# Moving the matmul operands of a one-core decoder layer to other places in the on-chip memory

## The chip, the cores and the metric

The kernel runs on one core of a Trainium2 chip. The metric is the device time of one execution in microseconds (us), the median of several runs. A profiled execution gives a page and a trace; its span runs from the first to the last instruction of the core.

## The reference

One post-norm decoder layer over 272 tokens (16 meta tokens and 256 others), width 2048, float32:

```
p = h @ W_in            # q | latent | index q | index key | index weights | pool channels
attn = sparse attention over the latent (64 best keys of each query, chosen by the index)
pool = trailing means (2, 4, 8, 16) less the token, mapped by group and scaled
h = LN(alpha * h + concat(attn, pool) @ W_o)
z = h @ w_up            # 2048 -> 2 * 5632
z = causal convolution of width 3 over the tokens, plus a bias
f = (gelu(a) * g) @ w_down          # a, g: the halves of z
h = LN(alpha * h + f)
```

## The kernel before

**Two parts, three products.** Every float32 operand of a large product is split into an upper part (rounded by ScalarE to the engine's faster float32 format, float32r) and a lower part (what is left, by VectorE). A product of activation and weight is then three matmuls that add up in PSUM: weight upper by activation upper (line 258), weight upper by activation lower (line 259), weight lower by activation upper (line 260). `product` issues these three for each of 16 blocks of 128 rows, 48 matmuls for one tile of 128 output channels. In all of them the weight is the stationary operand (loaded, 128x128) and the activation the moving one (streamed, 256 to 272 columns, 258 in most). In the down projection it is the other way round: `seven` and the "down" items stream 512 columns of weight over a loaded block of activation (lines 855 to 857 and 907 to 909).

**The weight tiles.** Weights come in 1 MB tiles. SyncE fetches a tile into `wraw` (three buffers); `split_part` makes the upper part on ScalarE (line 149) and the lower on VectorE (line 150), in two pieces of 1024 columns, into `whl` (three buffers). `weights` hands out the next tile and keeps two more in flight. `stream` is the order of the tiles: index queries, latent maps, queries, pool channels, output map, then the plan of the feed-forward part, in which up tiles and down tiles alternate.

**The activation slots.** The activations' two parts lie in `ring`, 24 slots of the tag "act": first `xp` (the input, 16 slots), then `mixa` and `mixp` (the input of the output map), then `hp` (the normalised activations, read by 80 up tiles), and `right` (gated activations of the down projection). The first eight up tiles read `fold` instead, activations before the normalisation, in 16 buffers of the pool `ffn`, which later hold the gated activations `gp`.

**Where they lie.** Class `Split` says where the parts of a weight tile start, class `Parts` where those of a slot start:

```
self.tile, self.places = tile, ((0, 1040), (2080, 3120)) if sums else ((0, 1024), (2080, 3104))
self.parts = flat[:, 6:6 + NQ], flat[:, 280:280 + NQ]
```

All places are in elements of 4 bytes. A slot is 2 x 272 elements, 2176 bytes or 8.5 times 256, so that neighbouring slots lie 128 bytes apart modulo 256. In a slot of `hp`, `mixa` or `mixp` the upper part starts 24 bytes in and the lower 1120. A weight tile has 4160 elements, 65 times 256 bytes, and so the three `whl` buffers start at one place modulo 256 (96 in the built program). Its four pieces start at 0 or at 128 modulo 256 from there: upper and lower of the first eight blocks at 0, of the other eight at 128. A block of 128 columns is 512 bytes, so that all blocks of a piece have that place. The buffers of `fold` and `gp` are 2080 bytes apart, which gives eight places modulo 256, 32 bytes apart.

The order of the work is the program's own on each engine, with edges (`issue_after`) that place some of VectorE's and ScalarE's instructions behind the split of a later tile. The reserved area at the start of the on-chip memory, 16384 bytes of each partition, holds the descriptors of the transfers that GpSimd issues.

Of the kernel before, what the change touches and what calls it, by code (L numbers as in the profile page):

```python
# [11 lines left out]
F32 = mybir.dt.float32  # L12
F32R = mybir.dt.float32r
# [4 lines left out]
P = 128  # L18
# [3 lines left out]
T = NM + S  # L22
Q0 = NM - 2
NQ = T - Q0
# [43 lines left out]
class Split:  # L68

    def __init__(self, tile, sums):

        self.tile, self.places = tile, ((0, 1040), (2080, 3120)) if sums else ((0, 1024), (2080, 3104))

    def __getitem__(self, key):
        rows, part, c = key
        a, b = c.start, 2 * 1024 + 2 if c.stop is None else c.stop
        at = int(a >= 1024)
        assert b <= 1024 or at == 1  # L80
        o = self.places[at][part] - 1024 * at
        return self.tile[rows, o + a:o + b]


class Parts:


    def __init__(self, slot):
        flat = slot.rearrange("p a b -> p (a b)")
        self.parts = flat[:, 6:6 + NQ], flat[:, 280:280 + NQ]  # L90

    def __getitem__(self, key):
        return self.parts[key[1]][key[0], key[2]]

K_PROJ = (1, 3, 5, 7, 9, 11, 13, 15, 0, 2, 4, 6, 8, 10, 12, 14)
K_O = (1, 3, 5, 7, 9, 10, 12, 14, 0, 2, 4, 6, 8, 11, 13, 15)
K_UP = (1, 3, 5, 7, 8, 10, 12, 15, 0, 2, 4, 6, 9, 11, 13, 14)  # L100
# [3 lines left out]
def tile_layer(ctx, tc, xt, w_first, w_proj, w_uk, w_uv, w_pool, w_o, w_up, w_down, cols, rows, rel_bias, onehot, out):  # L104
    nc = tc.nc
    sb = ctx.enter_context(tc.tile_pool(name="sb", bufs=1))
    wp = ctx.enter_context(tc.tile_pool(name="wp", bufs=3))
    ring = ctx.enter_context(tc.tile_pool(name="ring", bufs=24))
# [17 lines left out]
    stream = [w_proj[j] for j in range(8)] + [w_uk, w_uv] + [w_proj[j] for j in range(8, 24)]  # L126
    stream += [w_o[j] for j in range(KT)]
    plan = ffn_plan()
    kinds = {}
    for item in plan:  # L130
        if item[0] == "up":
            stream.append(w_up[item[2] * FT + item[1]])
        elif item[0] == "down":
            n = PARTS[FAST]
            stream.append(w_down[sum(PARTS[:FAST]) + n // 2 + (item[2] - 1) // 2 * (n // 4) + item[3]])
        else:
            kinds[len(stream)] = item[0]
            stream.append(w_down[sum(PARTS[:item[1]]) + item[2] * (PARTS[item[1]] // 2) + item[3]])
    stream += [w_down[d] for d in range(FT - PARTS[-1], FT)]
    spare, last = len(stream) - PARTS[-1], len(stream) - 1  # L140
    VALUES = stream.index(w_uv)
    ready, raws, split, held = {}, {}, {}, []
    state = {"next": 0, "use": 0}
# [26 lines left out]
            parts = split_part(raw, hl, slice(a, b))  # L170
        return parts

    def split_tile(sums=False):

        hl = Split(wp.tile([P, 4160], F32R, tag="whl", name="whl"), sums)
        if not state["use"]:

            wp.tile([P, 16], F32, tag="gap", name="gap", bufs=1)
        return hl

    def weight_tiles(sums=False):
        raw = wp.tile([P, 2048], F32, tag="wraw", name="wraw")
        return raw, split_tile(sums)

    def emit(i):
        if i in ready:
            return
        if i == last:

            raw = wp.tile([P, 2048], F32, tag="wraw", name="wraw")  # L190
            nc.sync.dma_start(raw, stream[i])
            raws[i] = raw
            ready[i] = []
            for c in range(0, 2048, 256):
                hl = ring.tile([P, 2, 258], F32R, tag="act", name="whl_r", padded_shape=[P, 2, T])
                nc.scalar.activation(hl[:, 0, :256], raw[:, c:c + 256], AF.Copy)
                nc.vector.tensor_tensor(hl[:, 1, :256], raw[:, c:c + 256], hl[:, 0, :256].bitcast(F32), op=ALU.subtract)
                ready[i].append(hl)
            return
        if i == spare:  # L200
            raw = wp.tile([P, 2048], F32, tag="wraw", name="wraw")
            hl = Split(sb.tile([P, 4160], F32R, tag="y", name="whl_y"), True)
        else:
            raw, hl = weight_tiles(i > spare)
        ready[i] = hl
        if i == VALUES:

            nc.sync.dma_start(raw, stream[i])
            held.extend((raw, hl))
            return  # L210
        split[i] = fetch(raw, hl, stream[i], kinds.get(i), i and i - 1 in split and split[i - 1][1])
        if i >= spare:
            raws[i] = raw
# [48 lines left out]
    at = ctx.enter_context(ExitStack())  # L262
# [4 lines left out]
    for k0, k1 in [(k, k + 1) for k in range(9)] + [(9, 12), (12, 15), (15, 16)]:  # L267
        if k0 == KT - 1:

            raw = ap_.tile([P, 1024], F32, name="wraw_l", tag="v1")[:, :T + MF].rearrange("p (a b) -> p a b", a=1)  # L270
        elif k0 % 3 == 0:
            raw = wp.tile([P, 2048], F32, tag="wraw", name="wraw")
            raw = raw[:, :3 * (T + MF)].rearrange("p (a b) -> p a b", b=T + MF)
        if k0 % 6 == 0:
            hl = split_tile()
        for w in ((slice(0, T), slice(T, T + MF)) if k0 == 0 else (slice(0, T + MF),)):
            nc.sync.dma_start(raw[:, k0 % 3:k0 % 3 + k1 - k0, w], w_first[k0:k1, :, w].rearrange("k p c -> p k c"))
        for k in range(k0, k1):
            xk, wk, a0 = raw[:, k % 3, :T], raw[:, k % 3, T:], k % 6 // 3 * 1024 + k % 3 * MF
            c = slice(a0, a0 + MF)  # L280
            a = ring.tile([P, 2, T], F32R, tag="act", name="xp")
            nc.scalar.activation(a[:, 0, :], xk, AF.Copy)
            nc.scalar.activation(hl[:, 0, c], wk, AF.Copy)
            nc.vector.tensor_tensor(a[:, 1, :], xk, a[:, 0, :].bitcast(F32), op=ALU.subtract)
            nc.vector.tensor_tensor(hl[:, 1, c], wk, hl[:, 0, c].bitcast(F32), op=ALU.subtract)
            x_parts.append(a)
            first.append((hl, c.start))
# [143 lines left out]
    for j in range(8):  # L431
        hl = weights()
# [10 lines left out]
        for i in range(2):  # L443
            r, o = slice(DI * i, DI * i + DI), slice(DI - DI * i, 2 * DI - DI * i)
# [27 lines left out]
    y = sb.tile([P, KT, T], F32, tag="y", name="x", padded_shape=[P, KT, T])  # L472
# [50 lines left out]
    for h in range(H):  # L523
        hl = weights()
# [65 lines left out]
    def values(h, pts, ptx):  # L590
        ps = small()
        hs = slice(h * HD, (h + 1) * HD)
        nc.tensor.matmul(ps[:, :NQ], vs[0][:, hs], ptx, start=True, stop=False)
        nc.tensor.matmul(ps[:, 2:NQ], vs[1][:, hs], pts[:, :2 * P], start=False, stop=False)
        nc.tensor.matmul(ps[:, 2 + P:NQ], vs[2][:, hs], pts[:, 2 * P:], start=False, stop=True)
        a = Parts(ring.tile([P, 2, T], F32R, tag="act", name="mixa"))
        nc.scalar.activation(a[:, 0, :NQ], ps[:, :NQ], AF.Copy)
        nc.vector.tensor_tensor(a[:, 1, :NQ], ps[:, :NQ], a[:, 0, :NQ].bitcast(F32), op=ALU.subtract)
        mix[h] = a
# [33 lines left out]
    def pooled(g, df, hl):  # L633
        for j in range(2):
            ps = small()
            for c in range(2):
                w = slice(256 * c + j * P, 256 * c + j * P + P)
                nc.tensor.matmul(ps[:, :NQ], hl[:, 0, w], df[:, c, 0, :], start=c == 0, stop=False)
                nc.tensor.matmul(ps[:, :NQ], hl[:, 0, w], df[:, c, 1, :], start=False, stop=False)
                nc.tensor.matmul(ps[:, :NQ], hl[:, 1, w], df[:, c, 0, :], start=False, stop=c == 1)  # L640
            m = 2 * g + j
            a = Parts(ring.tile([P, 2, T], F32R, tag="act", name="mixp"))
            nc.scalar.activation(a[:, 0, :NQ], ps[:, :NQ], AF.Copy, scale=col(G_POOL, m))
            nc.vector.scalar_tensor_tensor(a[:, 1, :NQ], ps[:, :NQ], col(G_POOL, m), a[:, 0, :NQ].bitcast(F32),
                                           op0=ALU.mult, op1=ALU.subtract)
            mix[8 + m] = a
# [5 lines left out]
    for h in range(H):  # L652
# [3 lines left out]
        hl = weights()  # L656
# [47 lines left out]
    sums = fp.tile([P, NQ + W], F32, name="sums", tag="u1", bufs=1)  # L704
# [64 lines left out]
    def normalise(m):  # L769
        yd = y[:, m, Q0:]  # L770
        nc.vector.tensor_tensor(yd, yd, rs, op=ALU.mult)  # L771
        nc.vector.tensor_tensor(yd, yd, m2, op=ALU.add)
        nc.scalar.activation(yd, yd, AF.Identity, bias=col(LN1, 2 * m + 1), scale=col(LN1, 2 * m))
        a = Parts(ring.tile([P, 2, T], F32R, tag="act", name="hp"))
        nc.scalar.activation(a[:, 0, :NQ], yd, AF.Copy)
        nc.vector.tensor_tensor(a[:, 1, :NQ], yd, a[:, 0, :NQ].bitcast(F32), op=ALU.subtract)  # L776
        h_parts.append(a)
# [45 lines left out]
    def forms(r, j, whole):  # L823
# [6 lines left out]
        nc.gpsimd.tensor_tensor(s[:, 3], a11, a21, op=ALU.subtract)  # L830
        left = two_parts(slot(), r[:, :, :P])
        mid = two_parts(slot(), s[:, :2])
        right = ring.tile([P, 2, T], F32R, tag="act", name="right")
        right = two_parts(right[:, :, :2 * P].rearrange("p a (b c) -> p a b c", c=P), s[:, 2:])
        if j % 2 == 0:
            held["lone"], held["other"] = slot(), slot() if whole else None
# [52 lines left out]
    for item in plan:  # L889
# [3 lines left out]
        if item[0] == "down":  # L893
            _, part, c, g = item
            hl = weights()
# [6 lines left out]
            n = PARTS[part]  # L902
# [18 lines left out]
        hl = weights()  # L921
# [233 lines left out]
```

## Time and profile before

| what | value |
|---|---|
| time, median of 3 runs | 1034.75 us (1034.6 to 1035.13) |
| span of the profiled execution | 1032.8 us |
| TensorE matmul busy | 1025.7 us, 99% |
| VectorE busy | 890.4 us, 86% |
| ScalarE busy | 622.4 us, 60% |
| GpSimd busy | 187.0 us, 18% |
| mean granted TensorE clock | 0.997 |
| moved by DMA | 250.28 MB, 242 GB/s |

The three runs lie 0.5 us apart. The span is 2.0 us under their median; a run's time has, beside the span, what lies before the first and after the last instruction. Matmuls overlap in TensorE's pipeline: a matmul's own duration (some 280 ns) is far longer than the distance from its start to the start of the next, and the busy time says only that something was in flight. The distance from start to start, called the pitch below, is what adds up to the time; it is read by counting starts in a stretch.

### The profile page before, as it was taken

To read this page: it belongs to the slowest core of one execution; us is meant where nothing else is said; L and a number is where in the kernel's file an instruction comes from. 1 tells how busy PE (TensorE), PEld (TensorE's weight loads), DVE (VectorE), ACT (ScalarE), POOL (GpSimd) and SP (SyncE) were. 2 spreads that over 40 slices of the span, in tenths; PEclk is the share of its full clock that TensorE was granted. 3 is DMA by queue.
4 is the path that set the end of the run, shared out by engine and by line. 5 is a ranking of instruction groups with operands and counts; after the bars stand their busy time and mean duration, and the time that the engine had idled before them with its cause. 6 is when DMAs were issued, how large, how long until landed. Compare 5 with 4: busy or idle time off the path is not lost.

```text
span 1032.8 us, 19199 instructions
## 1 busy us (share of the span) xinstructions
PE 1025.7 (99%) x7644; PEld 977.2 (95%) x7644; DVE 890.4 (86%) x1401; ACT 622.4 (60%) x1000; POOL 187.0 (18%) x245
## 2 busy tenths in 40 slices
PE   9999999999999999999999999999999999999997
PEld 8999999999999999999999999999999999999986
DVE  6878668758779998889999999999998999998976
ACT  7666446645448865655665555656556565565675
POOL 1200014125430022111121111211112111120031
PEclk9999999999999999999999999999999999999998
DMA  9755643454553569979887788877988878887875
GB/s 329 258 179 203 242 146 116 149 184 162 188 204 124 204 204 251 270 284 306 274 281 272 271 298 279 276 274 275 290 279 279 274 286 281 277 276 268 298 229 155
DMA packets 59754, 250.28 MB, mean 242 GB/s; under 512 B 21734, under 2 KB 22416, under 8 KB 32656
## 3 DMA queue, kind: packets, MB, share of 16 engines
q1 hardware_dynamic: 34592, 230.42, 61.7%
q0 software_dynamic: 7888, 16.14, 8.3%
q10 hardware_dynamic: 17184, 2.49, 1.5%
q8 instruction: 60, 0.98, 0.4%
q14 instruction: 30, 0.25, 0.1%
HBM read 232.50 MB, written 2.11 MB: 227 GB/s over the span
## 4 chain that ended last, share of the span: by engine, by line
PE 91%; DVE 4%; issue 2%; ACT 1%; POOL 1%; DMA 0%; SPq 0%; POOLq 0%; DVEq 0%; ACTq 0%
PE mm L260 22%; PE mm L258 22%; PE mm L259 22%; PE at L857 6%; PE at L856 6%; PE at L855 6%; PE mm L331 2%; DVE whl L150 1%; PE mm L909 1%; PE mm L908 1%; PE mm L907 1%; ACT whl L149 1%; DVE x L771 0%; DMA wraw<-in_w_first 0%; PE mm L559 0%
## 5 line engine op out<-in xcount | busy, mean ns | idle before, releaser
L150 DVE TENSOR_TENSOR whl<-wraw,whl 128x1024 fp32r<-128x1024 f32 (+1 forms) x416 | 486.8, 1205 | 35.7 <-ACT whl L149 34.7
L149 ACT ACTIVATE whl<-wraw 128x1024 fp32r<-128x1024 f32 (+1 forms) x416 | 403.1, 1015 | 108.1 <-DMA wraw<-in_w_up 21.4
L260 PE MATMUL mm<-hp,whl 128*128 128x258 f32 x1280 | 362.8, 283 | 0.0
L258 PE MATMUL mm<-hp,whl 128*128 128x258 f32 x1280 | 359.5, 281 | 0.0
L259 PE MATMUL mm<-hp,whl 128*128 128x258 f32 x1280 | 357.2, 279 | 0.3 <-DVE hp L776 0.3
L258 PEld LDWEIGHTS mm<-hp,whl 128*128 128x128 f32 x1280 | 243.8, 190 | 3.2
L259 PEld LDWEIGHTS mm<-hp,whl 128*128 128x128 f32 x1280 | 240.4, 188 | 3.7 <-DVE hp L776 0.5
L260 PEld LDWEIGHTS mm<-hp,whl 128*128 128x128 f32 x1280 | 240.2, 188 | 0.2
L258 PE MATMUL mm<-xp,whl 128*128 128x256 f32 (+5 forms) x384 | 111.3, 290 | 0.0
L260 PE MATMUL mm<-xp,whl 128*128 128x256 f32 (+5 forms) x384 | 108.6, 283 | 0.0
L259 PE MATMUL mm<-xp,whl 128*128 128x256 f32 (+5 forms) x384 | 108.5, 283 | 0.0
L790 ACT ACTIVATE z<-mm,cv 128x256 f32<-128x256 f32 x40 | 22.6, 566 | 91.1 <-PE mm L260 91.1
L827 POOL TENSOR_TENSOR forms<-za 128x128 f32<-128x128 f32 x20 | 21.9, 1093 | 306.2 <-DVE za L808 239.7
L258 PEld LDWEIGHTS mm<-xp,whl 128*128 128x128 f32 x384 | 72.3, 188 | 1.0 <-issue 0.5
L259 PEld LDWEIGHTS mm<-xp,whl 128*128 128x128 f32 x384 | 72.3, 188 | 0.4
L260 PEld LDWEIGHTS mm<-xp,whl 128*128 128x128 f32 x384 | 72.2, 188 | 0.0
L857 PE MATMUL at<-whl,gp 128*128 128x512 f32 x180 | 70.7, 394 | 0.0
L856 PE MATMUL at<-whl,gp 128*128 128x512 f32 x180 | 70.7, 394 | 0.0
L855 PE MATMUL at<-whl,gp 128*128 128x512 f32 x180 | 69.0, 393 | 0.0
L790 ACT ACTIVATE za<-mm,cv 128x256 f32<-128x256 f32 x40 | 22.7, 567 | 75.2 <-PE mm L260 66.9
L830 POOL TENSOR_TENSOR forms<-za 128x128 f32<-128x128 f32 x20 | 20.4, 1020 | 198.4 <-DVE za L808 184.5
L857 PEld LDWEIGHTS at<-whl,gp 128*128 128x128 f32 x180 | 33.8, 188 | 7.7
(349 smaller groups left out, 1888.1 us busy)
## 6 DMA issues: line engine op xcount, KB each, us to landing
wraw<-in_w_up SPq DMA_DIRECT2D x88, 1024.0 KB, 5.1
wraw<-in_w_down SPq DMA_DIRECT2D x80, 1024.0 KB, 6.6
wraw<-in_w_proj SPq DMA_DIRECT2D x24, 1024.0 KB, 5.1
wraw<-in_w_o SPq DMA_DIRECT2D x16, 1024.0 KB, 4.9
y<-v POOLq DMA_DIRECT2D x27, 256.0 KB, 8.2
y<-u POOLq DMA_DIRECT2D x18, 256.0 KB, 5.0
wraw<-in_w_first SPq DMA_DIRECT2D x8, 304.0 KB, 5.0
x<-in_xt SPq DMA_DIRECT2D x1, 2176.0 KB, 8.0
```

The costliest lines, as they stand in the source:

```text
L149: upper = nc.scalar.activation(hl[:, 0, c], raw[:, c], AF.Copy)
L150: lower = nc.vector.tensor_tensor(hl[:, 1, c], raw[:, c], hl[:, 0, c].bitcast(F32), op=ALU.subtract)
L258: nc.tensor.matmul(ps, wh, ah, start=n == 0, stop=False)
L259: nc.tensor.matmul(ps, wh, al, start=False, stop=False)
L260: nc.tensor.matmul(ps, wl, ah, start=False, stop=n == KT - 1)
L331: nc.tensor.matmul(ps[:m, :T], hl[:, t // 2, a0 + a:a0 + a + m], x_parts[k][:, t % 2, :], start=k == 0 and t == 0, stop=k == KT - 1 and t ...
L790: nc.scalar.activation(z, src[:, 2:NQ], AF.Identity, bias=col(C_B, j), scale=col(C_W, 3 * j + 2))
L827: nc.gpsimd.tensor_tensor(s[:, 0], a21, a22, op=ALU.add)
L830: nc.gpsimd.tensor_tensor(s[:, 3], a11, a21, op=ALU.subtract)
L855: nc.tensor.matmul(ps, a[:, 0, i], hl[:, 0, w], start=j == 0, stop=False)
L856: nc.tensor.matmul(ps, a[:, 0, i], hl[:, 1, w], start=False, stop=False)
L857: nc.tensor.matmul(ps, a[:, 1, i], hl[:, 0, w], start=False, stop=j == n - 1)
```

## The change

It moves operands and nothing else. A slot of the ring takes 2 x 288 elements, 2304 bytes or 9 times 256, so that all slots start at one place modulo 256. In a slot the upper part starts at byte 0 and the lower at 1088 for the blocks that stand in the first half of the weight tile (by the order K_UP), at 8 and 1104 for those in the second half. A weight tile takes 4352 elements (68 times 256 bytes); its upper part is one piece of 2048 columns and so is its lower part. The upper part of tile n starts 16 x (n modulo 16) bytes in, the lower part 8192 bytes later plus 0, 48, 96, 144 or 208 bytes, by n // 16 modulo 5. For the up tiles n counts from 72, so that the 80 up tiles that read `hp` are n = 80 to 159: each of the 16 x 5 places once. Other tiles take their number in the stream. The last four tiles, whose rows are also summed, have fixed places. The 64-byte gap behind the first weight buffer goes. The area for GpSimd's descriptors is 8192 bytes of each partition.

In the built program each engine has the same instructions in the same order as before, with the same shapes; only addresses differ. So no rows of the order are shown.

```diff
-    def __init__(self, tile, sums):
-        self.tile, self.places = tile, ((0, 1040), (2080, 3120)) if sums else ((0, 1024), (2080, 3104))
+    def __init__(self, tile, upper, lower):
+        self.tile, self.places = tile, (upper, lower)
...
-    def __init__(self, slot):
+    def __init__(self, slot, k):
         flat = slot.rearrange("p a b -> p (a b)")
-        self.parts = flat[:, 6:6 + NQ], flat[:, 280:280 + NQ]
+        (a, b) = ACTS[k in K_UP[8:]]
+        self.parts = flat[:, a:a + NQ], flat[:, b:b + NQ]
...
+WIDE = 288
+ACTS = ((0, 272), (2, 276))
+SHIFTS = (0, 12, 24, 36, 52)
+def places(n):
+    upper = 4 * (n % 16)
+    return upper, upper + 2048 + SHIFTS[n // 16 % 5]
...
         if item[0] == "up":
+            order_of[len(stream)] = n_up + 72
+            n_up += 1
...
-        hl = Split(wp.tile([P, 4160], F32R, tag="whl", name="whl"), sums)
-        if not state["use"]:
-            wp.tile([P, 16], F32, tag="gap", name="gap", bufs=1)
-        return hl
+        return Split(wp.tile([P, 4352], F32R, tag="whl", name="whl"), *where)
...
-            raw, hl = weight_tiles(i > spare)
+            raw, hl = weight_tiles((0, 2112) if i > spare else places(order_of.get(i, i)))
...
-            a = ring.tile([P, 2, T], F32R, tag="act", name="xp")
+            a = ring.tile([P, 2, T], F32R, tag="act", name="xp", padded_shape=[P, 2, WIDE])
...
-        a = Parts(ring.tile([P, 2, T], F32R, tag="act", name="hp"))
+        a = Parts(ring.tile([P, 2, WIDE], F32R, tag="act", name="hp"), m)
...
-    nc = _bacc.Bacc("TRN2", target_bir_lowering=False, num_devices=1)
+    nc = _bacc.Bacc("TRN2", target_bir_lowering=False, num_devices=1, dynamic_dma_scratch_size=8192)
```

## Rows read from the trace of the kernel before

**Rows 1.** The page: busy time, share of the span and instructions of each engine.

```profile
PE 1025.7 (99%) x7644; PEld 977.2 (95%) x7644; DVE 890.4 (86%) x1401; ACT 622.4 (60%) x1000; POOL 187.0 (18%) x245
```

**Rows 2.** The page: the chain that ended last, by engine and by line.

```profile
PE 91%; DVE 4%; issue 2%; ACT 1%; POOL 1%; DMA 0%; SPq 0%; POOLq 0%; DVEq 0%; ACTq 0%
PE mm L260 22%; PE mm L258 22%; PE mm L259 22%; PE at L857 6%; PE at L856 6%; PE at L855 6%; PE mm L331 2%; DVE whl L150 1%; PE mm L909 1%; PE mm L908 1%; PE mm L907 1%; ACT whl L149 1%; DVE x L771 0%; DMA wraw<-in_w_first 0%; PE mm L559 0%
```

**Rows 3.** Waits of TensorE: who waited for whom, total us, times, longest.

```profile
PE at L1045 <- ACT diag L1043: 1.5, 1, 1.5
PE at L123 <- PEq L1144: 0.8, 1, 0.8
PE mm L331 <- ACT whl L283: 0.4, 2, 0.2
PE mm L259 <- DVE hp L776: 0.3, 1, 0.3
```

**Rows 4.** Stretches, TensorE alone: bounds, length, busy (instructions), granted clock, DMA share, GB/s.

```profile
92.42:138.33 45.91, 45.91 (x385) 1.00 0.51 181
243.70:301.16 57.46, 57.46 (x482) 1.00 0.52 181
308.77:348.90 40.13, 40.13 (x338) 1.00 0.46 158
372.19:400.63 28.44, 28.44 (x243) 1.00 0.83 222
```

**Rows 5.** The same of the feed-forward part, all of TensorE's matmuls, then those of `hp` alone.

```profile
450.00:950.00 500.00, 500.00 (x3601) 1.00 0.83 281
...
450.00:950.00 500.00, 358.69 (x2947) 1.00 0.83 281
```

**Rows 6.** Matmuls in order of time near 500 us: start, duration, engine, line.

```profile
499.40 0.39 PE L855 MATMUL at<-whl,right 128*128 128x512 f32 x1
...
500.79 0.40 PE L855 MATMUL at<-whl,gp 128*128 128x512 f32 x1
501.02 0.39 PE L856 MATMUL at<-whl,gp 128*128 128x512 f32 x1
501.25 0.40 PE L857 MATMUL at<-whl,gp 128*128 128x512 f32 x1
501.49 0.28 PE L258 MATMUL mm<-hp,whl 128*128 128x258 f32 x1
```

**Rows 7.** Groups with shapes kept apart: count, busy us, mean ns, idle time before.

```profile
L260 PE MATMUL mm<-hp,whl 128*128 128x258 f32 x1280 | 362.8, 283 | 0.0
L258 PE MATMUL mm<-hp,whl 128*128 128x258 f32 x1280 | 359.5, 281 | 0.0
L259 PE MATMUL mm<-hp,whl 128*128 128x258 f32 x1280 | 357.2, 279 | 0.3 <-DVE hp L776 0.3
L258 PE MATMUL mm<-fold,whl 128*128 128x260 f32 x128 | 36.3, 284 | 0.0
L260 PE MATMUL mm<-mixp,whl 128*128 128x258 f32 x128 | 36.2, 283 | 0.0
L857 PE MATMUL at<-whl,gp 128*128 128x512 f32 x180 | 70.7, 394 | 0.0
```

**Rows 8.** All engines, 450 to 950 us: busy of PE, PEld, DVE, ACT, POOL.

```profile
450.00:950.00 500.00, 500.00 (x3601) 471.54 (x3601) 462.17 (x634) 301.08 (x420) 81.97 (x97) 1.00 0.83 281
```

**Rows 9.** The split of weight tiles and a transfer issued by GpSimd, 450 to 950 us.

```profile
L150 DVE TENSOR_TENSOR whl<-wraw,whl 128x1024 fp32r<-128x1024 f32 x246 | 278.1, 1171 | 5.1 <-ACT whl L149 4.7
...
L149 ACT ACTIVATE whl<-wraw 128x1024 fp32r<-128x1024 f32 x246 | 232.7, 999 | 53.4 <-DMA wraw<-in_w_up 19.6 <-DVE wraw L161 19.1 <-DVE wraw L166 12.0
...
L884 POOL DMA_DIRECT2D y<-v x8 | 9.6, 1202 | 0.0
```

**Rows 10.** The page: transfers that GpSimd issues, count, KB each, us to landing.

```profile
y<-v POOLq DMA_DIRECT2D x27, 256.0 KB, 8.2
y<-u POOLq DMA_DIRECT2D x18, 256.0 KB, 5.0
```

More of the change, by code (lines that the diff above doesn't have):

```diff
@@ L68 @@
 class Split:
-    def __init__(self, tile, sums):
-        self.tile, self.places = tile, ((0, 1040), (2080, 3120)) if sums else ((0, 1024), (2080, 3104))
+    def __init__(self, tile, upper, lower):
+        self.tile, self.places = tile, (upper, lower)
     def __getitem__(self, key):
         rows, part, c = key
[L78 to L82, printed above, removed]
+        o = self.places[part]
+        return self.tile[rows, o + c.start:o + (2 * 1024 + 2 if c.stop is None else c.stop)]
 class Parts:
-    def __init__(self, slot):
+    def __init__(self, slot, k):
         flat = slot.rearrange("p a b -> p (a b)")
-        self.parts = flat[:, 6:6 + NQ], flat[:, 280:280 + NQ]
+        (a, b) = ACTS[k in K_UP[8:]]
+        self.parts = flat[:, a:a + NQ], flat[:, b:b + NQ]
     def __getitem__(self, key):
         return self.parts[key[1]][key[0], key[2]]
+WIDE = 288
[4 more added lines that the diff above has]
+    return upper, upper + 2048 + SHIFTS[n // 16 % 5]
 K_PROJ = (1, 3, 5, 7, 9, 11, 13, 15, 0, 2, 4, 6, 8, 10, 12, 14)
@@ L128, in tile_layer @@
     plan = ffn_plan()
-    kinds = {}
+    kinds, order_of, n_up = {}, {}, 0
     for item in plan:
         if item[0] == "up":
+            order_of[len(stream)] = n_up + 72
+            n_up += 1
             stream.append(w_up[item[2] * FT + item[1]])
@@ L171, in fetch, with split_tile, weight_tiles @@
         return parts
-    def split_tile(sums=False):
-        hl = Split(wp.tile([P, 4160], F32R, tag="whl", name="whl"), sums)
-        if not state["use"]:
-            wp.tile([P, 16], F32, tag="gap", name="gap", bufs=1)
-        return hl
-    def weight_tiles(sums=False):
+    def split_tile(where=(0, 2048)):
+        return Split(wp.tile([P, 4352], F32R, tag="whl", name="whl"), *where)
+    def weight_tiles(where):
         raw = wp.tile([P, 2048], F32, tag="wraw", name="wraw")
-        return raw, split_tile(sums)
+        return raw, split_tile(where)
     def emit(i):
@@ L194, in emit @@
             for c in range(0, 2048, 256):
-                hl = ring.tile([P, 2, 258], F32R, tag="act", name="whl_r", padded_shape=[P, 2, T])
+                hl = ring.tile([P, 2, 258], F32R, tag="act", name="whl_r", padded_shape=[P, 2, WIDE])
                 nc.scalar.activation(hl[:, 0, :256], raw[:, c:c + 256], AF.Copy)
@@ L201, in emit @@
             raw = wp.tile([P, 2048], F32, tag="wraw", name="wraw")
-            hl = Split(sb.tile([P, 4160], F32R, tag="y", name="whl_y"), True)
+            hl = Split(sb.tile([P, 4160], F32R, tag="y", name="whl_y"), 0, 2056)
         else:
-            raw, hl = weight_tiles(i > spare)
+            raw, hl = weight_tiles((0, 2112) if i > spare else places(order_of.get(i, i)))
         ready[i] = hl
@@ L595, in values @@
         nc.tensor.matmul(ps[:, 2 + P:NQ], vs[2][:, hs], pts[:, 2 * P:], start=False, stop=True)
-        a = Parts(ring.tile([P, 2, T], F32R, tag="act", name="mixa"))
+        a = Parts(ring.tile([P, 2, WIDE], F32R, tag="act", name="mixa"), h)
         nc.scalar.activation(a[:, 0, :NQ], ps[:, :NQ], AF.Copy)
@@ L641, in pooled @@
             m = 2 * g + j
-            a = Parts(ring.tile([P, 2, T], F32R, tag="act", name="mixp"))
+            a = Parts(ring.tile([P, 2, WIDE], F32R, tag="act", name="mixp"), 8 + m)
             nc.scalar.activation(a[:, 0, :NQ], ps[:, :NQ], AF.Copy, scale=col(G_POOL, m))
@@ L832, in forms @@
         mid = two_parts(slot(), s[:, :2])
-        right = ring.tile([P, 2, T], F32R, tag="act", name="right")
+        right = ring.tile([P, 2, T], F32R, tag="act", name="right", padded_shape=[P, 2, WIDE])
         right = two_parts(right[:, :, :2 * P].rearrange("p a (b c) -> p a b c", c=P), s[:, 2:])
```

## The prediction

> **What bounds the kernel now.** I read the page's busy times first, then the chain, TensorE's waits, and last the stretches in which starts can be counted. TensorE has a matmul in flight for 99% of the span [rows 1]; 91% of the chain is TensorE's, nearly all of it in the three lines of `product` (258 to 260) and the three of `seven` (855 to 857) [rows 2]. All its waits together are 3.0 us [rows 3]. So the kernel is a queue of matmuls, and its time is the sum of their pitches. A change that leaves every instruction and its order as they are, as this one does, can act on the time in one way only: by the pitch of equal matmuls.
>
> Does the pitch depend on where operands lie? The groups cannot tell: their durations are 279 to 284 ns for any 258 or 260 columns [rows 7], more than twice the pitch. The stretches can. Each stretch in [rows 4] holds whole products of 48 back to back; of the counts printed, the one to three above a multiple of 48 were in flight at its start. The queries take 45.91 us for 384, a pitch of 119.6 ns; the output map 57.46 us for 480, 119.7 ns; the first up tiles, which read `fold` and have 260 columns, 40.13 us for 336, 119.4 ns; up tiles that read `hp` 28.44 us for 240, 118.5 ns. The clock is 1.00 in all of them, the 2.4 GHz level, and TensorE waits for nothing. The DMA share is higher in the fastest stretch (0.83) than in the slow ones (0.46 to 0.52), so traffic is not what slows them.
>
> From 450 to 950 us, 500 us hold some 2945 matmuls on `hp` and 654 of 512 columns [rows 5]. Nine of the latter run from 499.40 to 501.49 us, 232 ns each [rows 6]; that leaves (500 - 654 x 0.232) / 2945 = 118.2 ns for `hp`, and with 118.5 from the stretch above I take 118.4. A column costs (232 - 118.4) / 254 = 0.45 ns, so `fold` at 258 columns would have 119.4 - 0.9 = 118.5. Equal work thus runs at 118.4 to 119.7 ns in one program; what differs is where the operands lie and in which order blocks follow each other. That is the size of effect that the rows bear out: about 1%.
>
> The Trainium skill speaks against any effect. Its page "TensorE: Matmul & The Clock Gate" says, in the section on what happens when you issue a matmul, that loading the next weights goes through a read port of its own and takes nothing from the running matmul, and in the section on the back-to-back gap it puts the gap at N / 2.4 + 2.5 ns, an estimate of 110 ns for 258 columns. The trace disagrees with the second (118.4 to 119.7 ns); by the first the change would be worth nothing. I keep that as a rival.
>
> **The change part by part.**
> *Matmuls on `hp`, 80 tiles x 48 = 3840* (1280 for each of three lines) [rows 7]. They leave one fixed pattern of places, 118.4 ns, for 16 x 5 patterns, each met once, so the new pitch is an average over patterns. The trace has no such tile, so I bound it by the nearest rows. `fold` comes closest in kind: its 16 buffers already lie at eight places modulo 256, so its 118.5 is an average as well. The queries and the output map, 119.6 and 119.7, show what other patterns can cost. Midway is 119.1: +0.7 ns x 3840 = **+2.7 us**. The ends: 117.8 (as far below 118.4 as `fold`'s middle way lies from the slow stages, 0.6) gives -2.3 us; 119.7 gives +5.0 us.
> *Queries and output map, 24 tiles, 1152 matmuls.* They too get scattered weights, and slots that all start alike. From 119.65 to 119.1: -0.55 x 1152 = **-0.6 us**; the ends are -1.3 us (118.5) and 0.
> *`fold`, index queries and pool channels, 384 + 768 matmuls.* The first keep their activations where they were modulo 256 up to one common step, and are an average already; the others mix with short matmuls of other kinds and give no clean stretch. 0, with 0.6 ns either way: 0.7 us.
> *Matmuls of 512 columns, about 900.* Here the weight streams. It lay at two places and now lies at many; the loaded activation lay at eight places and still does. 0, with 1 ns either way (two ends that the 0.45 ns of two columns would also make): 0.9 us.
> *The split on VectorE and ScalarE.* The same pieces of 1024 columns go to other addresses [rows 9]. Nothing prices a place for these engines. VectorE is busy 462 of 500 us in the feed-forward part [rows 8], so 38 us are free there; 246 lower parts of 1171 ns would have to grow by 38 / 246 = 0.15 us, 13%, before TensorE had to wait. Taken as 0.
> *Half the descriptor area.* GpSimd's transfers are few: 45 accumulations into `y` of 256 KB [rows 10], each taking some 1.2 us of GpSimd to issue [rows 9], and GpSimd is busy 18% [rows 1]. If the area were too small, GpSimd would hold a transfer back until an older one lands, 5 to 8 us [rows 10]; up to 38 us of idle VectorE and 418 of idle GpSimd time in 500 cover that [rows 8]. Taken as 0.
> *Code for the last tiles, the gap behind the first buffer:* addresses only, 0.
>
> The sum is +2.7 - 0.6 = +2.1 us on the profiled span of 1032.8. Nearly all of the span is the chain that moves, so it goes on the median unshortened: 1034.75 + 2.1 = **1036.9 us**. A difference of 0.2%, 2.07 us, is about what a measurement of this kernel can tell from no change; the forecast is just beyond it.
>
> **The rivals.**
> *Nothing that can be measured.* Either places don't matter, as the rule above has it, and the stages differ by their order alone; or the average over patterns comes out like `fold`, 118.5: +0.1 x 3840 = +0.4 and -0.6 from the other stages. Both give 1034.5 to 1034.8. For it speaks that `fold` is the only stage read here that is scattered; against it, that two stages out of four are 1% slower with the same instructions. Chance 0.33.
> *Faster: the new places avoid a clash in most matmuls.* The excess over a pure 0.45 ns per column is what a clash could be: 118.4 - 258 x 0.45 = 2.3 ns by that price; in the best case all 3840 lose it, -8.8 us, and the other 1152 with them lose as much again beside their own 1.2 ns, -4.0 us: 1022. With half the matmuls spared it is about 1028.4. It decides once the mean pitch on `hp` falls below 118.0 (with the 0.6 us of the other stages). For it speaks that all slots now start at one place, so that each pattern is regular; against it, that the weights visit all 16 places, good and bad alike. Chance 0.20.
> *Much slower: some patterns clash in every matmul.* If a third of the tiles ran at 3 ns above the middle way, hp would gain another 1.0 x 3840 = 3.8 us: 1040.7. Chance 0.07.
> *Another engine becomes the bound.* If VectorE's lower parts grew by 20% through their places, 246 x (0.23 - 0.15) = 20 us in 500 would come on the path: about 1055. Or a transfer of GpSimd held back 8 us near the end, where `finish_first` needs it: 1043. Chance 0.03 together. That the change doesn't move what it says is excluded by the addresses in the built program.
>
> **How the numbers follow.** Forecast 0.37, the two slower rivals 0.10: slower by over 0.2% 0.47; within 0.2% 0.33; faster by over 0.2% 0.20. The forecast's own ends are -2.3 - 1.3 - 0.7 - 0.9 = -5.2 us and +5.0 + 0 + 0.7 + 0.9 = +6.6 us, if all fell one way. The range takes in most of these: from 1031.0, which leaves out the better part of the faster rival, to 1041.5, which takes in a third of the tiles clashing. About 0.17 is left outside.
>
> **What would show it.** Right: the same counts, clock 1.00, waits of TensorE still near 3 us, and in the stretch from 450 to 950 us some 15 to 20 fewer matmuls than 3599 (500 us divided by a mean pitch 0.6% longer); up tiles at different pitches, one from the next, from 117 to 121 ns, each constant within its tile; queries and output map at or under 119.5 ns. Wrong: equal pitches in all 80 tiles (places don't matter); a mean on `hp` under 118 or over 120; new waits of TensorE on VectorE's line for the lower part, or a hole near the end behind a transfer of GpSimd.

## The result and the profile after

The changed kernel takes 1042.48 us, the median of 3 runs (1042.28 to 1043.03), against 1034.75: 1.0075 times the time, 95% interval 1.0055 to 1.0095. It is slower, and by more than forecast. The profiled execution has a span of 1040.5 us, 7.7 us more than before.

The page has the same 19199 instructions; its first part, with busy time, share of the span and instructions of each engine:

```profile
PE 1032.6 (99%) x7644; PEld 983.9 (95%) x7644; DVE 889.6 (85%) x1401; ACT 621.4 (60%) x1000; POOL 186.6 (18%) x245
```

Beside [rows 1], TensorE's matmuls grew by 6.9 us and its weight loads by 6.7 at equal counts; the other engines did not grow. TensorE's waits are no longer than before, 2.5 us in all against 3.0, and the one that is new takes 0.2 us. They are, as in [rows 3] (line numbers are some lines higher in this kernel):

```profile
PE at L1050 <- ACT diag L1048: 1.5, 1, 1.5
PE at L130 <- PEq L1149: 0.8, 1, 0.8
PE mm L1067 <- DVE whl L254: 0.2, 1, 0.2
```

So the time went into the pitch. The stretches that answer to [rows 4] (bounds, length, busy with count, clock, DMA share, GB/s), and behind them two single up tiles, the slowest and the fastest:

```profile
92.22:137.99 45.77, 45.77 (x385) 1.00 0.51 180
243.61:301.42 57.81, 57.81 (x482) 1.00 0.52 180
309.01:349.26 40.25, 40.25 (x338) 1.00 0.45 160
372.77:401.62 28.85, 28.85 (x242) 1.00 0.81 226
650.43:656.35 5.92, 5.92 (x49) 1.00 0.75 268
897.17:902.86 5.69, 5.69 (x50) 1.00 0.75 216
```

Divided by 384, 480, 336 and 240 starts: queries 119.2 ns (119.6 before), output map 120.4 (119.7), `fold` 119.8 (119.4), up tiles on `hp` 120.2 (118.5). The two single tiles run at 5.92 / 48 = 123.3 and 5.69 / 48 = 118.5 ns: the same instructions and the same clock; what the program sets differently is the weight's place. In the feed-forward stretch of [rows 5] there are 3568 matmuls instead of 3601, first all of them, then those on `hp`:

```profile
450.00:950.00 500.00, 500.00 (x3568) 1.00 0.84 277
...
450.00:950.00 500.00, 361.05 (x2926) 1.00 0.84 277
```

The mean over all starts on `hp` in the trace (distances over 140 ns left out, here and below) is 118.42 ns before and 120.16 after. 1.74 ns x 3840 = 6.7 of the 7.7 us.

A yardstick for all kernels below is the stretch from the first matmul of the eleventh up tile on `hp` to the first of the eightieth: 69 up tiles (3312 matmuls on `hp`) and the same 727 matmuls of 512 columns in every trace. It takes 560.39 us before and 566.46 after:

```profile
410.91:971.30 560.39, 560.39 (x4041) 1.00 0.83 280
```
```profile
412.01:978.47 566.46, 566.46 (x4040) 1.00 0.84 277
```

### The profile page after: what moved, and what is told of

It is laid out like the page before. It is cut to its first block, busy times and chain, and to the rows that moved or that the text cites. A ratio compares the mean times of both kernels' runs of the same rounds, so it can differ in the third digit from the quotient of the medians.

```text
span 1040.5 us, 19199 instructions
## 1 busy us (share of the span) xinstructions
PE 1032.6 (99%) x7644; PEld 983.9 (95%) x7644; DVE 889.6 (85%) x1401; ACT 621.4 (60%) x1000; POOL 186.6 (18%) x245
## 4 chain that ended last, share of the span: by engine, by line
PE 89%; DVE 5%; issue 2%; DMA 1%; POOL 1%; ACT 1%; SPq 0%; POOLq 0%; DVEq 0%; ACTq 0%
PE mm L265 22%; PE mm L264 22%; PE mm L263 22%; PE at L861 6%; PE at L860 6%; PE at L862 6%; DVE whl L159 2%; PE mm L336 2%; DMA wraw<-in_w_down 1%; DVE x L776 0%; DVE hp L781 0%; POOL gb L979 0%; DMA wraw<-in_w_first 0%; PE mm L564 0%; ACT whl L158 0%
```

## The experiments

Three theories were on the table. Theory 1: the scatter of the weights as such costs. Theory 2: the slots' new places cost. Theory 3: only the pair counts, where the loaded weight lies against the streamed activation. For theory 3 the changed kernel is itself a table: its 80 up tiles have 80 places, and each half of a tile has another slot layout. The means by tile and half, read from it, gave the numbers expected below. (A half is the first or the last eight of a tile's 16 blocks; a block is three matmuls.) One tile is one sample, which will matter.

### Slots alone

The weight pieces go back to 0 and 128 modulo 256.

```diff
-    def __init__(self, tile, upper, lower):
-        self.tile, self.places = tile, (upper, lower)
+    def __init__(self, tile, sums):
+        self.tile, self.places = tile, ((0, 1040), (2080, 3120)) if sums else ((0, 1024), (2080, 3104))
...
-            raw, hl = weight_tiles((0, 2112) if i > spare else places(order_of.get(i, i)))
+            raw, hl = weight_tiles(i > spare)
```

> The changed kernel with the weight tiles back at their former places (0 and 128 modulo 256, upper and lower part of a block alike); slots, descriptor area and all else as changed. Theory 1 (the scattered weights alone cost the 7.7 us): mean pitch on hp back at 118.4 ns, 1035 us. Theory 2 (the slots' new places cost it): near 120.2 ns, 1042 us. Theory 3 (only the pair of places counts, slot against weight): the changed kernel's own tiles with upper at 0 and lower at distance 0 ran the first eight blocks at 121.5 ns, those with upper at 128 and distance 0 the other eight at 119.4, so every tile here runs at about 120.5 ns, all 80 alike, 1043 us.

Measured: 1042.36 us, 1.0072 (1.0057 to 1.0087); 120.30 ns on `hp`, the first halves of the tiles at 121.27 and the second at 119.33. The yardstick:

```profile
411.93:978.84 566.91, 566.91 (x4041) 1.00 0.83 277
```

With the old weight places the kernel is as slow as the change, so theory 1 falls. Theory 2 would give the total as well, but not the halves: 121.5 and 119.4 were expected from the pairs, 121.27 and 119.33 came. The tiles are not quite alike, though theory 3 expected that: they run from 119.2 to 120.8 ns.

### Weights alone

```diff
-ACTS = ((0, 272), (2, 276))
+ACTS = ((6, 280), (6, 280))
...
-        a = Parts(ring.tile([P, 2, WIDE], F32R, tag="act", name="hp"), m)
+        a = Parts(ring.tile([P, 2, T], F32R, tag="act", name="hp"), m)
```

The other slots go back in the same way, and so does the gap.

> The changed kernel with the slots back at 2176 bytes, parts 24 and 1120 bytes in, and the 64-byte gap back in front of them; the weight tiles scattered as in the change. Theory 1 (weights): about 1042.5 us, 120.2 ns on hp. Theory 2 (slots): 1035 us, 118.4 ns. Theory 3 (the pair): an average over pairs again, 119.5 to 120.5 ns, 1039 to 1043 us, spread from tile to tile.

Measured: 1040.88 us, 1.0065 (1.0048 to 1.0082); 119.84 ns on `hp`, single tiles from 118.6 to 121.5.

```profile
411.84:977.12 565.28, 565.28 (x4041) 1.00 0.83 278
```

The old slots don't bring the time back either, and theory 2 falls. Either half of the change, alone, costs nearly all of it: the two are not added up but pair up.

### Half the descriptor area alone

```diff
-    nc = _bacc.Bacc("TRN2", target_bir_lowering=False, num_devices=1)
+    nc = _bacc.Bacc("TRN2", target_bir_lowering=False, num_devices=1, dynamic_dma_scratch_size=8192)
```

> The kernel before with only the descriptor area halved. All three theories of places: 1034.7 us, since all addresses move by 8192 bytes together. Rival (GpSimd's transfers are held back, or places count beyond 256 bytes): over 1036.8 us.

Measured: 1035.09 us, 1.0003 (0.9993 to 1.0012), 118.41 ns. Half the area costs nothing, and moving all addresses down by 8192 bytes changes nothing.

```profile
412.25:972.63 560.38, 560.38 (x4040) 1.00 0.83 280
```

### The worst place for all up tiles

```diff
-            raw, hl = weight_tiles((0, 2112) if i > spare else places(order_of.get(i, i)))
+            raw, hl = weight_tiles((0, 2112) if i > spare else ((28, 2100) if i in order_of and order_of[i] >= 80 else places(order_of.get(i, i))))
```

> The changed kernel with all 80 up tiles that read hp at the place whose own tile was slowest there: upper part 112 bytes in, lower part 96 further (123.4 ns in the one tile that had it). If the place makes the pitch: all 80 at 123.4 ns, 3840 x 3.2 = 12.4 us more than the change, 1055 us. If the tile's turn or its neighbours make it: 120.2 ns on average, 1042.5 us.

Measured: 1054.06 us, 1.0184 (1.0169 to 1.0199); 123.41 ns, every tile between 122.3 and 124.0.

```profile
413.75:990.81 577.06, 577.06 (x4040) 1.00 0.81 273
```

One place, given to 80 tiles, takes its pitch to all of them: 3.25 ns over the change, x 3840 = 12.5 us; the spans of the two profiled executions differ by 12.0 us and the median times by 11.6. For this place the tile's turn and its data are out.

Another rival can be looked up in this trace: the change also moves where VectorE and ScalarE write the parts of the weights while TensorE runs, and the pitch could depend on those writes. The line below (bounds, length, then busy time of the engines as in [rows 8]) holds the starts of 12 matmuls in the last blocks of a tile, with VectorE, ScalarE and GpSimd idle throughout:

```profile
994.82:996.31 1.49, 1.49 (x14) 1.49 (x13) 0.00 (x0) 0.00 (x0) 0.00 (x0) 1.00 1.00 423
```

They start 124.4 ns apart, as slow as such blocks are while the other engines work (124.4 ns). The slow pitch does not need the other engines.

### All buffers moved by 64 bytes

On the kernel with half the area, so that it fits:

```diff
+    sb.tile([P, 16], F32, name="pad")
     wp = ctx.enter_context(tc.tile_pool(name="wp", bufs=3))
```

> The kernel before with half the descriptor area and every buffer 64 bytes further, weights and slots alike. If only the distance between the pair of operands counts (modulo 256): 118.4 ns on hp and 1035 us, as before. If each operand's own place counts: another pitch, 119 to 121 ns, 1037 to 1044 us.

Measured: 1035.58 us, 1.0000 (0.9991 to 1.0010); 118.42 ns, and tile by tile the pitches of the kernel before to 0.1 ns.

```profile
411.56:971.95 560.39, 560.39 (x4041) 1.00 0.84 280
```

The yardstick is equal to 0.01 us. A move of 64 bytes that both operands make together does not count.

### The kernel before without its gap

```diff
-        if not state["use"]:
-            wp.tile([P, 16], F32, tag="gap", name="gap", bufs=1)
```

> The kernel before without the 64-byte gap behind the first weight buffer: all slots 64 bytes nearer to the weights, nothing else. Pair theory: a new pair, so another pitch, by the spread of the changed kernel's tiles between 118 and 122 ns, most likely 120 (1041 us). Rival (the scatter as such is what costs, a fixed pair is cheap): 118.4 ns, 1035 us.

Measured: 1041.71 us, 1.0059 (1.0042 to 1.0076); 119.63 ns, nearly all tiles at 119.3 to 119.8, six at 120.9.

```profile
412.42:977.27 564.85, 564.85 (x4041) 1.00 0.83 278
```

The same 64 bytes, now between the pair: 0 us when both move, +4.5 us on the yardstick when one does. A fixed pair is not cheap by being fixed; the one of the kernel before was a good one.

### The best place for all up tiles

As in the worst place, with (20, 2120) for (28, 2100).

> The changed kernel with all 80 up tiles that read hp at the place whose own tile was fastest there on the mean of its two halves: upper part 80 bytes in, lower part 208 further (117.8 ns in the first eight blocks, 119.0 in the others). Pair theory: 118.4 ns on hp, 3840 x 1.8 = 6.9 us less than the change, 1035.5 us. If the tile's turn made it: 120.2 ns, 1042.5 us.

Measured: 1038.21 us, 1.0025 (1.0016 to 1.0034); 118.93 ns, 0.5 over what was expected, tiles at two levels, 118.5 to 119.0 and 119.4 to 119.8. The direction holds (4.3 us under the change), the size does not: 1035.5 us was expected. The two levels come from the first half of the tiles: once settled (blocks five to eight), 55 tiles run at 117.8 ns there and 25 at 120.0.

```profile
410.97:973.45 562.48, 562.48 (x4041) 1.00 0.84 280
```

### The best place for each half

```diff
+        if len(self.places) == 4 and c.start >= 1024:
+            o = self.places[2 + part] - 1024
...
+            raw, hl = weight_tiles((0, 2112) if i > spare else ((20, 1160, 2320, 3460) if i in order_of and order_of[i] >= 80 else places(order_of.get(i, i))))
```

A weight tile takes 4544 elements here, 71 times 256 bytes.

> The same with four pieces again, so that each half of a tile has its own place: first eight blocks as in best_place (117.8 ns), the other eight with the upper part at 64 and the lower 208 further (118.0 ns in its tile of the changed kernel). Piece starts keep their place modulo 512. Pair theory: 117.9 ns on hp, 3840 x 0.5 = 1.9 us under the kernel before on hp; with the output map's 0.7 us more: 1033.7 us. If a half's pitch depends on what the other half does: 118.5 ns or more, 1036 us.

Measured: 1036.17 us, 1.0005 (0.9995 to 1.0015), where 1033.7 was expected; 118.31 ns on `hp`, first halves 118.70 (expected 117.8), second halves 117.93 (expected 118.0).

```profile
412.42:973.06 560.64, 560.64 (x4041) 1.00 0.83 280
```

The second half came out, the first did not. The starts by block show why. The first three blocks of a half are still settling: the first eight blocks here run at 119.8, 119.5, 119.0, 118.4, 118.2, 118.2, 118.2, 118.1 ns in the mean over the tiles. And that mean hides two levels: from the fifth block to the eighth, 64 tiles run at 117.8 ns and 16 at 119.9. The first half's pair had been picked as the fastest of 80 single samples. In that one tile it ran at 117.7 to 118.0 ns from its first block on, without settling and at the lower level; so what ran ahead of it was part of its 117.8.

The slots of the settled blocks lie at both places modulo 512 bytes, and it makes no difference, which agrees with 256 bytes as the period. Whether 128 bytes would make one was not tried.

### One pair for whole tiles

```diff
-ACTS = ((0, 272), (2, 276))
+ACTS = ((2, 276), (2, 276))
...
-            raw, hl = weight_tiles((0, 2112) if i > spare else places(order_of.get(i, i)))
+            raw, hl = weight_tiles((0, 2112) if i > spare else (16, 2116) if i in order_of and order_of[i] >= 80 or 26 <= i < 26 + KT else (4, 2064) if 10 <= i < 18 else places(order_of.get(i, i)))
```

> The changed kernel with one layout in every slot of hp, mixa and mixp (upper part 8 bytes in, lower at 1104) and one place for the 80 up tiles and the 16 output tiles (upper 64 bytes in, lower 208 further): the pair that ran the second half of every tile of best_pieces at 117.9 ns. The eight query tiles take the place at which the changed kernel ran its fastest one (upper 16 in, lower 48 further, 117.7 ns). Pair theory: hp 117.8 ns (-0.6 x 3840 = -2.4 us against the kernel before), output map 117.9 (-1.3 us), queries 117.7 (-0.7 us): 1030.5 us, faster than both kernels. If what runs ahead of a block counts as well (the first half of a tile set the state in which the second ran): the pair settles at another pitch, 118.5 to 119.5 ns, 1034 to 1038 us.

Measured: 1034.51 us, 0.9997 (0.9988 to 1.0006). Queries 117.80 ns (117.7 expected), the output map 118.5 (117.9 expected). But `hp` has a mean of 118.49 and two levels: most tiles at 117.7 to 118.6, twenty at 119.8 to 121.1. Two tiles of equal place, within 9 us of each other:

```profile
661.36:667.17 5.81, 5.81 (x49) 1.00 1.06 288
669.95:675.61 5.66, 5.66 (x50) 1.00 0.84 314
```

5.81 / 48 = 121.0 and 5.66 / 48 = 117.9 ns. So the pair alone does not fix the pitch: this pair has more than one settled level. Of the first nine tiles, which follow one another without a down tile between, none is at the upper level; all twenty come later, where matmuls of 512 columns stand between the tiles. That what runs ahead chooses the level is argued from this order, not tried, and those matmuls can't be all of it: in best_place the third, fifth, seventh and ninth tiles are at the upper level with none of them ahead.

The kernel before has two levels as well. Settled in the first half of a tile, 75 of its 80 tiles run at 117.9 ns and five at 122.1. Two first halves of 24 matmuls, of the 29th and the 30th tile:

```profile
558.63:561.47 2.84, 2.84 (x26) 1.00 0.26 40
566.38:569.30 2.92, 2.92 (x26) 1.00 1.01 334
```

By their starts these are 118.3 and 121.8 ns. The five are the same tiles (11, 30, 38, 47 and 55) in the traces of the kernel before, of scratch_alone and of all_moved. So the level is not chance: something that these three kernels share sets it, and moving all operands together leaves it.

### Another pair for whole tiles

As above, with (12, 2096) for (16, 2116).

> The same with upper 48 bytes in and lower 144 further for the up and output tiles: the pair whose second half ran at 118.04 ns in one tile of the changed kernel, and in that alone. Pair theory: 118.1 ns, 1031.5 us. If a single tile's pitch also holds what ran ahead of it: 118 to 119.5 ns with two or more levels among equal tiles, 1031.5 to 1037 us.

Measured: 1031.47 us, 0.9961 (0.9948 to 0.9975), faster than both kernels: 3.7 us under the runs of the kernel before beside it (1035.21). `hp` at 117.95 ns, all tiles between 117.7 and 118.5; output map 117.9, queries 117.8. That is the time that was expected (1031.5 us), and only the lower level occurs.

```profile
408.47:967.80 559.33, 559.33 (x4041) 1.00 0.84 280
```

Its blocks start at 119.0, 118.2, 118.1 ns and then stay at 117.8, in the three lines of `product` 121.7, 114.2 and 117.5. The second halves of best_pieces, with another pair, settled at 121.6, 114.2 and 117.5: two pairs, one settled pitch. Here too 12 settled matmuls run with the other engines idle, 117.8 ns apart by their starts:

```profile
387.94:389.36 1.42, 1.42 (x15) 1.42 (x14) 0.00 (x0) 0.00 (x0) 0.00 (x0) 1.00 0.89 189
```

No up tile of any kernel here has a mean under 117.67 ns.

## Why the prediction was wrong

**What held.** That the time is a sum of pitches, and that the change can act on nothing else: counts and clock are the same, the waits differ by 0.5 us, and 6.7 of 7.7 us are the pitch on `hp`. That the places decide: no_gap against all_moved and worst_place against best_place show it. That tiles would differ among each other, by the forecast from 117 to 121 ns: 118.4 to 123.4. That the descriptor area and the split on VectorE are free: scratch_alone is at 1.0003, and VectorE's busy time fell by 0.8 us. Of the signs given for being right, three failed: the pitch is not constant within a tile, the output map is at 120.4 ns and not under 119.5, and the stretch from 450 to 950 us lost 33 matmuls, not 15 to 20; one of the signs of being wrong, a mean on `hp` over 120, came.

**The step that failed** is the first term, the new pitch on `hp`: 119.1 ns forecast (+2.7 us), 120.16 measured (+6.7 us), beyond the end of 119.7 that was given as the upper bound. Two choices made it. The bound was taken from two stages of the kernel before as if they showed the cost of bad places; the runs show stages at 119.6 to 119.7 to be nothing bad: the mean over the 80 new pairs is 120.16, over those of weights_alone 119.84, a pair shifted by 64 bytes 119.63. And `fold` (118.5) was taken for a fair average of places; it moves little when the weights scatter (119.4 to 119.8 ns for 260 columns). It has eight places but one fixed distance between its two parts, which may be why; that was not tried. What the rows read did not show is that the pair of the kernel before was among the best of those tried: 79 of the 80 tiles of the changed kernel are slower than its mean of 118.42 ns, and in 75 of its own 80 tiles it settles at 117.9 ns in the first half (at 122.1 in five), where the best found settles at 117.8.

**The second term**, -0.6 us from queries and output map, had the wrong sign for the larger part: queries gained 0.4 ns (-0.1 us), the output map lost 0.7 (+0.5 us). The sum, +0.4 us, lies outside the bounds given for it, -1.3 us to 0. `fold` cost 0.1 us and the matmuls of 512 columns 0.5 ns each, 0.4 us; these are within their bounds.

**The rivals.** "Nothing that can be measured" fell: between best_place and worst_place, with the same loads and streams, the pitch on `hp` went from 118.93 to 123.41 ns by the weight's places alone. The rule behind it in the prediction is that of the Trainium skill, page "TensorE: Matmul & The Clock Gate", section "What happens when you issue a matmul", that loading the next weights takes no read bandwidth from the running matmul. The measured pitch does not follow from this rule; whether the load takes the time from the stream, no run shows. The 110 ns that the prediction quotes from the Trainium skill, the same page, section "Back-to-back issue gap", is given there for an isolated matmul, not for a stream of loads and matmuls, so the 118.4 to 119.7 ns of the trace are no disagreement with that section. "Faster: a clash avoided" fell for the change; its sign, a mean on `hp` under 118.0, came only in other_pair (117.95), and that a clash is what was avoided there is not shown. "Much slower: a third of the tiles clash" came nearest in time: 1040.7 us, with a chance of 0.07; it ended short of the result, as did the range (1041.5). Its mechanism did not occur: one tile of 80, not a third, ran 3 ns above the forecast's 119.1, and 79 tiles ran above the kernel before, by 1.7 ns in the mean of all. Untried places can be worse than any in the trace: the upper bound had to lie beyond the slowest stage seen (119.7), not at it.

**What stays open.** It is open why the distance counts. The loading of one block and the streaming for the block before it could meet in the memory; that would fit a pitch that depends on the distance between the two and on nothing that moves both, but no run took one of the two away. What sets the level at which a pair settles wasn't tried either.

## What to carry to other kernels

Where matmuls run back to back and TensorE waits for nothing, count starts in a stretch of the trace: the pitch differed by 5% between tiles of equal shape (117.7 to 124.0 ns). A matmul's own duration is easy to overlook as a sign: between the kernel before and worst_place its mean rose by the same 5 ns, but from 281 to 286, under 2%. What counted here is where the streamed operand lies against the loaded one: 64 bytes less between the two cost 6 us, and a step of 256 bytes from one slot to the next made no difference. So a buffer added or dropped between them can change the time, and a kernel whose pair is a good one, as here, has more to lose than to gain by an untried move. A table of many places in one run is a cheap way to look, but its best entries are single samples: run a candidate alone, in all tiles, before believing it.

## What was not expected of the hardware

- The pitch of an fp32r matmul of 258 columns behind a load of 128x128 ran from 117.7 to 124.0 ns by tile, at granted clock 1.00, with no wait in the trace.
- A distance of 64 bytes between the operands' buffers cost 4.5 us in 560; moving both by 64 or by 8192 bytes cost 0.01 us.
- The stream settles within three or four blocks of three matmuls, and one pair of places can settle at two levels: 117.8 and 120.0 to 121.2 ns in one_pair, 117.9 and 122.1 in the kernel before, there in the same five tiles of 80 in three traces.
- The pitch of settled blocks in worst_place was 124.4 ns with VectorE, ScalarE and GpSimd idle, and the same with them at work.
